# Shifting where the moving operands of matmuls begin in memory, modulo 256 bytes, against the weights

## The chip, the core and the metric

The kernel runs on one NeuronCore of a Trainium2 chip. TensorE (PE in the profile) multiplies; VectorE (DVE), ScalarE (ACT) and GpSimd (POOL) do the element-wise work; SyncE (SP) issues most of the DMAs. SBUF is the on-chip memory of 128 partitions that the operands lie in, and PSUM takes the matmuls' sums. The metric is the device time of one execution, in microseconds. The kernel before takes 3229.51 us (median of 3 runs, 3228.76 to 3231.86).

## What is computed

Two models run one after the other on a sequence of 256 tokens with 1024 features, all in float32. The first has two layers, each a mixer (a long convolution, a gated linear attention and a pooling branch, merged by three gates) and a gated feed-forward net of width 2816. The second has four layers (neighbourhood attention, a convolution module, a short gated convolution, attention again), each followed by a squared-ReLU MLP of width 4096; in its first three layers a second stream of 256 context tokens goes along. Cut to what matters:

```python
for i in range(2):                                   # first model
    h = _rms_norm(x, norm_mix_pre[i]); proj = h @ w_in[i]
    ...                                              # three branches, three gates
    x = x + _rms_norm(merged @ w_out[i], norm_mix_post[i])
    a, b = _split(_rms_norm(x, norm_ffn_pre[i]) @ ffn_w_up[i], (D_FF, D_FF))
    y = (gelu(_dwconv3_centred(a, ...)) * b) @ ffn_w_down[i]
    x = x + _rms_norm(y, norm_ffn_post[i])
for i in range(4):                                   # second model, streams x and ctx
    x = x + mod_l[:, 2] * mixer_i(modulate(rmsnorm(x, norm1_g[i]), ...))
    x = x + mod_l[:, 5] * (square(relu(m_l @ mlp_w1[i])) @ mlp_w2[i])
```

## The kernel before

**Layout.** Features lie on the 128 partitions and tokens along the free dimension, so a gemm has weights of 128 x 128 float32 as the stationary operand and 256 or 512 tokens as the moving one. In the first model and in the last layer's MLP and attention queries a moving operand has 256 columns (one stream); in the second model's layers 0 to 2 it mostly has 512 (both streams). At some tails and heads of layers 0 to 2 (`by_stream`, `head_tiles`) the two streams are done one after the other, with 256 columns each.

**Three matmuls for one.** Every float32 number is held as a rounded high part and a low part. `mm3` makes one product of three matmuls: high weights by high activations (line 142), high by low (147), low by high (148). Each matmul comes with its own weight load (LDWEIGHTS, PEld in the profile), which runs beside the matmul before it. A gemm over 1024 features is a chain of 8 contraction tiles, 24 matmuls, into one PSUM bank.

```python
i = nc.tensor.matmul(out, wh, xh, start=start, stop=False, skip_group_check=True)
...
    nc.tensor.matmul(out, wh, xl, start=False, stop=False, skip_group_check=True)
    nc.tensor.matmul(out, wl, xh, start=False, stop=stop, skip_group_check=True)
```

**Weights.** `load_w` fetches 1 MB of weights by SP's queue into `raw` (two buffers), ScalarE rounds them into `whi` (line 128) and VectorE takes the rest into `wlo` (line 130), 1024 elements a partition at a time, in rings of four buffers. A buffer is free again when PE is through with it.

**Moving operands.** `ah`, `al` (8 x 512 per partition) hold the normalized activations of every stage; the first model uses their first 256 columns as the gemms' operand and the other 256 for two of its branches (`branch`). `yph`, `ypl` are the third branch; `hh`, `hl` the operand of the feed-forward's down gemm and of `w_out`; `mhh`, `mhl` that of the MLPs' second gemm; `vh`, `vl`, `uh`, `ul`, `soh`, `sol` those of the output gemms of the attention, the convolution module and the short convolution; `Ph`, `Pl` the attention's weights by head, which move against `vh`, `vl` as stationary operand. In the value gemms (`w_v`, `att_v`) the roles are turned: `whi`, `wlo` move with 512 columns, and `ah`, `al` are stationary.

**Order.** A tile framework allots addresses and puts waits; each engine runs its instructions in program order. Pools are stacks: a tile that is put in front of another moves its address and nothing else. The mixer's steps (`STEPS`) and the attention's loop over pairs of heads leave VectorE and ScalarE work between gemms; gates, feed-forward nets and MLPs are long runs of gemms.

Of the kernel before, what the change touches and what calls it, by code (L numbers as in the profile page):

```python
# [11 lines left out]
F32R = mybir.dt.float32r  # L12
# [6 lines left out]
P = 128  # L19
T = 256  # L20
KD = 8
NL1 = 2
NL2 = 4
# [12 lines left out]

STEPS = (("h", 0), ("z", 0), ("h", 1), ("z", 1), ("h", 2), ("z", 2), ("h", 3), ("z", 3),
         ("p", 0), ("x", 0), ("x", 1), ("p", 1), ("g", 0), ("g", 1))


_VEC = {}
# [38 lines left out]
class Kern:  # L80
# [13 lines left out]
    def t(self, pool, tag, shape, dt=F32, bufs=None):  # L94
        kw = {} if bufs is None else {"bufs": bufs}
        return pool.tile(list(shape), dt, tag=tag, name=self.nm(tag), **kw)

    def ps(self, tag="mm", dt=F32):
        return self.psum.tile([P, 512], dt, tag=tag, name=self.nm(tag), bufs=self.psbufs[tag])
# [160 lines left out]
    def setup(self):  # L260
        nc, a = self.nc, self.a
        self.cp = self.pool("cp", bufs=1)
        self.wp = self.pool("wp", bufs=1)
        self.psbufs = {"mm": 2, "ko": 4, "mi": 1, "mo": 1}
        self.psum = self.pool("ps", bufs=1, space=PSUM)
        self.X = self.t(self.cp, "X", [P, 2, KD, T])
        self.vec = self.t(self.cp, "vec", [P, _NV])
        with self.tc.high_priority():
            self.ordered(self.vec[:, :NV1], a["vecs"][:, :NV1])
            self.ordered(self.X[:, 0, 0:4], a["x"][:, 0:4])  # L270
        self.ident = self.t(self.cp, "ident", [P, P])
        self.lead = [(self.X[:, 0, 4:8], a["x"][:, 4:8]), (self.ident, a["ident"])]
        self.ones = self.t(self.cp, "ones", [P, P])
        nc.vector.memset(self.ones, 1.0)
        self.inv = {}
        for nd in (P, DM):
            self.inv[nd] = self.t(self.cp, f"inv{nd}", [P, 2])
            nc.vector.memset(self.inv[nd], 1.0 / nd)
        self.mhalf = self.t(self.cp, "mhalf", [P, 4])
        nc.vector.memset(self.mhalf, -0.5)  # L280
        self.one1 = self.t(self.cp, "one1", [P, 1])
        nc.vector.memset(self.one1, 1.0)
        self.mod = [self.t(self.cp, f"mod{l}", [P, 2, 48]) for l in range(NL2)]
        self.sc = self.t(self.cp, "sc", [P, KD, 32])
        nc.vector.memset(self.sc, 0.0)
        nc.gpsimd.memset(self.mod[NL2 - 1], 0.0)
        self.mod_done = 0
        self.mroom = None
        self.mods = self.mod_bursts()

        self.main = self.pool("main", bufs=1)
        self.ah = self.t(self.main, "ah", [P, KD, 512], F32R)
        self.al = self.t(self.main, "al", [P, KD, 512], F32R)

    def silu_c(self):
        nc = self.nc
# [83 lines left out]
    def run(self, out):  # L380
        nc, a, X = self.nc, self.a, self.X
        with ExitStack() as st:
            self.f1 = self.pool("f1", st, bufs=1)
            with ExitStack() as mx:
                self.b1 = b1 = self.pool("mx", mx, bufs=1)
                self.mroom = b1, 2
                self.dft = self.t(b1, "dft", [P, 4, 2, P])
                self.cnt = self.t(b1, "cnt", [P, 4, 2, 8])
                self.smask = self.t(b1, "smask", [P, T])
                nc.vector.memset(self.smask, 1.0)  # L390
                nc.vector.memset(self.smask.rearrange("p (c t) -> p c t", t=P)[:, :, 0:1], 0.0)
                self.lmask = self.t(b1, "lmask", [P, P], U32)
                update = self.ffn(0, self.mixer(0, None))
                update = self.mixer(1, update)
            self.mp = self.pool("mix0", st, bufs=1)
            vs = self.att_v(0, 0)
            update = self.ffn(1, update, lambda: next(vs))
            norm = self.norm0
            acc = self.t(self.main, "sacc", [P, T], bufs=1)
            for m in range(KD):  # L400
                update(m)
                sq = acc if not m else self.t(self.main, "s2", [P, T], bufs=6)
                self.mark = nc.scalar.activation(sq, X[:, 0, m], AF.Square).ins
                if 0 < m < KD - 1:
                    nc.gpsimd.tensor_tensor(acc, acc, sq, ALU.add)
            self.norm_stream(norm, 0, [acc, sq])
            nxt = []
            self.attention(0, 0, norm, vs, True, self.behind(0, nxt))
        with ExitStack() as st:
            self.mp = self.pool("mlp0", st, bufs=1)  # L410
            norm = self.mlp(0, 512, nxt[0])
        for l in range(1, NL2):
            norm = self.layer2(l, norm)
        for k in range(0, KD, 2):
            eng = (nc.sync, nc.scalar)[k // 2 % 2]
            eng.dma_start(out[:, k : k + 2], X[:, 0, k : k + 2])
# [13 lines left out]
    def prenorm1(self, g, update=None):  # L430

        nc, X = self.nc, self.X
        xh, xl = self.ah[:, :, :T], self.al[:, :, :T]
        for k in range(KD):
            if update:
                update(k)
            gk = self.v(g, k)
            self.mark = nc.scalar.activation(xh[:, k], X[:, 0, k], AF.Copy, scale=gk).ins
            nc.vector.scalar_tensor_tensor(xl[:, k], X[:, 0, k], gk, xh[:, k].bitcast(F32), ALU.mult, ALU.subtract)  # L439
        acc = self.sumsq([X[:, 0, 2 * k : 2 * k + 2] for k in range(4)], self.main)  # L440
        rt, rp = self.rstd([q[:, j] for q in acc for j in range(2)], DM, self.main)
        r = self.t(self.main, "rs", [P, T], bufs=2)
        nc.scalar.copy(r, rp)
        return xh, xl, r, rt
# [66 lines left out]
    def branch(self, q, n=1):  # L511

        if q < KD:
            return tuple(x[:, q : q + n, T:] for x in (self.ah, self.al))
        return tuple(x[:, q - KD : q - KD + n] for x in self.yp)

    def filter_time(self, h, w3, tag):
# [36 lines left out]
    def mixer(self, i, update):  # L554
# [112 lines left out]
        for m in range(KD):  # L667
# [4 lines left out]
            for b in range(3):  # L672
                dst = psl[b // 2][:, b % 2]
                for k in range(KD):
                    wh, wl = lg[b]
# [37 lines left out]
                ctx = self.norm_context()  # L713
            if i + 1 == NL1 and m == KD - 1:
                for k in range(KD):
                    self.shift_split(self.norm0[0], k, 1, ctx[:, k])
            if m:
                out(*pend)
            pend = (m, mh, ml)
# [246 lines left out]
    def norm_open(self, l, which):  # L966

        nc, mod = self.nc, self.mod[l]
        s0 = 24 * which
        gs = self.t(self.main, "gs", [P, 2, 8], bufs=2)  # L970
        nc.vector.scalar_tensor_tensor(
            gs, mod[:, :, s0 + 8 : s0 + 16], 1.0,
            self.v(f"norm{which + 1}_g{l}", 0, 8)[:, None, :].to_broadcast([P, 2, 8]), ALU.add, ALU.mult,
        )
        return mod[:, :, s0 : s0 + 8], gs, self.ah, self.al

    def shift_split(self, sh, k, s, t):
        ah, al = (x[:, k, s * T : (s + 1) * T] for x in (self.ah, self.al))
        b = sh[:, s, k : k + 1]
        self.nc.scalar.activation(ah, t, AF.Identity, bias=b)  # L980
        self.nc.vector.scalar_tensor_tensor(al, t, b, ah.bitcast(F32), ALU.add, ALU.subtract)  # L981

    def norm_stream(self, norm, s, parts):
        nc, X = self.nc, self.X
        sh, gs, ah, al = norm
        _, rp = self.rstd(parts, DM, self.main)
        r = self.t(self.main, "rs", [P, T], bufs=2)
        nc.scalar.copy(r, rp)
# [1 line left out]
        for k in range(KD):  # L990
            t = self.t(self.main, "s2", [P, 512], bufs=6)[:, :T]
            nc.vector.scalar_tensor_tensor(t, X[:, s, k], gs[:, s, k : k + 1], r, ALU.mult, ALU.mult)
            self.shift_split(sh, k, s, t)

    def head_tiles(self, src, cnt, xh, xl, n, tag="ko", order=(0, 1)):

# [101 lines left out]
    def mlp(self, l, n, norm):  # L1098
        nc, a = self.nc, self.a
        _, _, mh, ml = norm  # L1100
        if l + 1 < NL2:
            self.spread_c()
        s1 = self.tiles(a["mlp_w1"][l])
        s2 = self.tiles(a["mlp_w2"][l])
        nxt = []
# [41 lines left out]
    def att_v(self, l, slot):  # L1147

        mp, a = self.mp, self.a
        v = [self.t(mp, tag, [P, 4, DM], F32R) for tag in ("vh", "vl")]  # L1150

        def weights(n2):
# [6 lines left out]
        def group(ws, n2, tts, tags):  # L1159
            pv = [self.ps(tag) for tag in tags]  # L1160
            for kk in range(KD):
                wh, wl = (w[:, kk % 2] for w in ws[kk // 2])
                for ps, tt in zip(pv, tts):
                    s = slice(tt * P, (tt + 1) * P)
                    self.mm3(ps, self.ah[:, kk, s], self.al[:, kk, s], wh, wl, kk == 0, kk == KD - 1)
            return lambda: [
                self.split(*(q[:, tt, n2 * 512 : (n2 + 1) * 512] for q in v), ps) for ps, tt in zip(pv, tts)
            ]
# [19 lines left out]
    def attention(self, l, slot, norm, vs, live, done):  # L1188
# [63 lines left out]

        def values(hp, S, st):
            nk = 4 if st == 0 else 2
            ph = []
            for h in range(2):
                Ph = self.t(mp, "Ph", [P, 4, T], F32R, bufs=2)
# [51 lines left out]
    def conformer(self, l, norm, done):  # L1309
# [103 lines left out]
        nc.gpsimd.tensor_tensor(r, var, self.mhalf, ALU.pow)  # L1413
        nc.vector.scalar_tensor_tensor(nm, mu, -1.0, r, ALU.mult, ALU.mult)
        rb, nb = self.spread(r, "mi"), self.spread(nm, "mm")
        uh = self.t(mp, "uh", [P, KD, 512], F32R)
        ul = self.t(mp, "ul", [P, KD, 512], F32R)
        for m in range(KD):
# [8 lines left out]
    def short(self, l, norm, done):  # L1427
        nc, a, mp = self.nc, self.a, self.mp
        _, _, ah, al = norm
        src = self.tiles(a["sc_win"])  # L1430
        W = T + 2
        oh = self.t(mp, "soh", [P, KD, 512], F32R)
        ol = self.t(mp, "sol", [P, KD, 512], F32R)
        for m in range(KD):
# [238 lines left out]
```

## Time and profile before

| | before |
|---|---|
| median of 3 runs | 3229.51 us (3228.76 to 3231.86) |
| profiled execution | 3229.86 us |
| its span (first to last instruction) | 3228.1 us |
| PE busy | 3122.4 us, 97% |
| DVE busy | 2140.7 us, 66% |
| ACT busy | 1498.2 us, 46% |
| mean granted clock of PE | 0.982 |

A matmul's record begins when its columns begin to enter; its end is modelled, so one record overlaps the next, and the pace of a run of matmuls is the distance from start to start. Busy time of PE is the union of these records.

### The profile page before, as it was taken

The numbers are of one execution on the slowest core, as the hardware profiler recorded it, in microseconds if no ns is written. First come the engines' busy times: TensorE is split into PE (matmuls) and PEld (weight loads), VectorE is DVE, ScalarE is ACT, GpSimd is POOL, SyncE is SP. The second block draws the span as 40 slices with busy tenths as digits, with TensorE's granted clock in tenths as the row PEclk, the third lists the DMA queues.
The fourth block names the chain that finished last, engine by engine and source line by source line (L and its number), as shares of the span: only waits on it lengthen the run. The fifth ranks groups of instructions, "written<-read, shape, count | busy, mean of one in ns | idle before, by whom it ended". The sixth has DMA issues, their size and how long they took to land.

```text
span 3228.1 us, 46918 instructions
## 1 busy us (share of the span) xinstructions
PE 3122.4 (97%) x18954; PEld 2707.5 (84%) x18954; DVE 2140.7 (66%) x3445; ACT 1498.2 (46%) x2371; POOL 226.6 (7%) x219
## 2 busy tenths in 40 slices
PE   8899999989999999999999899999999999999998
PEld 6699898889899778888886588888888888787898
DVE  6876666786776566898358869943547843446655
ACT  5344445444544576433346553333334333346654
POOL 0200000020101100000006500000000000110000
PEclk9899999999999999999999899999999999999999
DMA  8345565445454221575221137722234832222354
GB/s 287 121 163 183 178 227 200 163 145 182 163 183 157 92 79 46 173 238 189 96 88 66 40 109 236 236 98 92 92 105 157 299 105 92 97 92 95 121 183 144
DMA packets 81337, 469.12 MB, mean 145 GB/s; under 512 B 9364, under 2 KB 9802, under 8 KB 37088
## 3 DMA queue, kind: packets, MB, share of 16 engines
q1 hardware_dynamic: 78768, 460.01, 42.0%
q0 software_dynamic: 1328, 4.31, 0.4%
q8 instruction: 149, 2.44, 0.3%
q10 hardware_dynamic: 1024, 1.81, 0.2%
q14 instruction: 68, 0.56, 0.1%
HBM read 465.04 MB, written 1.05 MB: 144 GB/s over the span
## 4 chain that ended last, share of the span: by engine, by line
PE 65%; issue 23%; DVE 7%; ACT 2%; POOL 1%; DMA 1%; SPq 0%; POOLq 0%; DVEq 0%; ACTq 0%
PE ko L142 9%; PE ko L147 9%; PE mm L142 9%; PE ko L148 9%; PE mm L147 9%; PE mm L148 9%; DVE wlo L130 2%; ACT whi L128 1%; PE mm L1262 1%; PE mo L142 1%; PE mo L147 1%; PE mo L148 1%; DVE mm L1387 1%; PE mi L224 1%; POOL nms L228 1%
## 5 line engine op out<-in xcount | busy, mean ns | idle before, releaser
L128 ACT CAST whi<-raw 128x1024 fp32r<-128x1024 f32 (+2 forms) x676 | 699.1, 1037 | 1212.5 <-PE mm L147 677.8
L130 DVE TENSOR_TENSOR wlo<-raw,whi 128x1024 fp32r<-128x1024 f32 (+2 forms) x656 | 797.1, 1218 | 416.8 <-ACT whi L128 411.7
L142 PE MATMUL ko<-ah,whi 128*128 128x512 f32 (+1 forms) x1536 | 545.0, 356 | 3.7 <-ACT ah L980 3.0
L147 PE MATMUL ko<-al,whi 128*128 128x512 f32 (+1 forms) x1536 | 544.2, 355 | 1.3 <-DVE al L981 1.3
L148 PE MATMUL ko<-ah,wlo 128*128 128x512 f32 (+1 forms) x1536 | 543.4, 355 | 0.0
L142 PE MATMUL mm<-ah,whi 128*128 128x256 f32 (+1 forms) x1744 | 509.2, 292 | 23.2 <-DVE s L464 20.5
L148 PE MATMUL mm<-ah,wlo 128*128 128x256 f32 (+1 forms) x1744 | 505.2, 290 | 0.8 <-DVE wlo L130 0.8
L147 PE MATMUL mm<-al,whi 128*128 128x256 f32 (+1 forms) x1744 | 504.8, 289 | 0.4 <-DVE al L439 0.4
L142 PEld LDWEIGHTS mm<-ah,whi 128*128 128x128 f32 x1744 | 337.9, 194 | 44.0 <-issue 30.1
L147 PE MATMUL mm<-mhl,whi 128*128 128x512 f32 (+1 forms) x952 | 345.5, 363 | 0.3
L142 PE MATMUL mm<-mhh,whi 128*128 128x512 f32 (+1 forms) x952 | 345.3, 363 | 0.0
L148 PE MATMUL mm<-mhh,wlo 128*128 128x512 f32 (+1 forms) x952 | 345.0, 362 | 0.0
L148 PEld LDWEIGHTS mm<-ah,wlo 128*128 128x128 f32 x1744 | 337.5, 194 | 6.3 <-DVE wlo L130 1.8
L147 PEld LDWEIGHTS mm<-al,whi 128*128 128x128 f32 x1744 | 337.8, 194 | 5.8 <-issue 1.6
L142 PEld LDWEIGHTS ko<-ah,whi 128*128 128x128 f32 x1536 | 290.2, 190 | 45.2 <-ACT ah L980 3.7
L353 DVE SCALAR_TENSOR_TENSOR mjunk<-mraw,cb 128x1024 f32<-128x1024 f32 x256 | 312.7, 1222 | 20.1 <-DMA mraw<-in_mod_w_dram 14.6
L147 PEld LDWEIGHTS ko<-al,whi 128*128 128x128 f32 x1536 | 290.6, 189 | 41.2 <-DVE al L981 1.7
L148 PEld LDWEIGHTS ko<-ah,wlo 128*128 128x128 f32 x1536 | 290.4, 189 | 39.6 <-issue 0.2
L147 PEld LDWEIGHTS mm<-mhl,whi 128*128 128x128 f32 x952 | 178.3, 187 | 33.6 <-DVE mhl L205 1.5
L1022 DVE SCALAR_TENSOR_TENSOR X<-mm,mod,X 128x256 f32<-128x256 f32 x206 | 92.8, 479 | 171.2 <-PE mm L148 171.2
L142 PEld LDWEIGHTS mm<-mhh,whi 128*128 128x128 f32 x952 | 178.3, 187 | 32.2
L148 PEld LDWEIGHTS mm<-mhh,wlo 128*128 128x128 f32 x952 | 178.3, 187 | 32.0
(396 smaller groups left out, 5066.4 us busy)
## 6 DMA issues: line engine op xcount, KB each, us to landing
raw<-in_mlp_w_dram SPq DMA_DIRECT2D x128, 1024.0 KB, 4.9
mraw<-in_mod_w_dram SPq DMA_DIRECT2D x144, 512.0 KB, 4.3
raw<-in_w_in_dram SPq DMA_DIRECT2D x52, 1024.0 KB, 4.9
raw<-in_w_up_dram SPq DMA_DIRECT2D x44, 1024.0 KB, 4.9
mraw<-in_mod_w_dram SPq DMA_DIRECT2D x24, 1024.0 KB, 4.9
raw<-in_w_down_dram SPq DMA_DIRECT2D x22, 1024.0 KB, 4.9
raw<-in_na_qk_dram SPq DMA_DIRECT2D x16, 1024.0 KB, 4.8
raw<-in_w_br_dram SPq DMA_DIRECT2D x16, 768.0 KB, 4.3
```

The costliest lines, as they stand in the source:

```text
L128: nc.scalar.copy(hi[:, :step], raw[:, s])
L130: eng.tensor_tensor(lo[:, :step], raw[:, s], hi[:, :step].bitcast(F32), ALU.subtract)
L142: i = nc.tensor.matmul(out, wh, xh, start=start, stop=False, skip_group_check=True)
L147: nc.tensor.matmul(out, wh, xl, start=False, stop=False, skip_group_check=True)
L148: nc.tensor.matmul(out, wl, xh, start=False, stop=stop, skip_group_check=True)
L224: nc.tensor.matmul(*args, start=False, **kw)
L228: nc.gpsimd.tensor_tensor(y, x, self.mhalf[:, :nch], ALU.pow)
L353: nc.vector.scalar_tensor_tensor(junk, w, 1.0, self.cb[:, r], ALU.mult, ALU.mult, accum_out=mod[:, r, n : n + 1])
L1022: nc.vector.scalar_tensor_tensor(X[:, s, m], ps[:, sl], self.mod[l][:, s, 8 * gate + m : 8 * gate + m + 1], X[:, s, m], ALU.mult, ALU.add)
L1262: nc.tensor.transpose(pt[:, kt * P : (kt + 1) * P], S[2 * h + qt][:, kt * P : (kt + 1) * P], self.ident)
L1387: nc.vector.scalar_tensor_tensor(d, u[:, :, j : j + T], tap(j), d, ALU.mult, ALU.add)
```

## The change

Nothing is computed otherwise: the built program has the same instructions on every engine, in the same order and with the same waits. What differs is where tiles lie. The weights `whi` and `wlo` begin at 192 modulo 256 bytes in every contraction tile, before and after (a tile of weights is 512 bytes long, so this holds for each). Below, "at" means that a moving operand begins at the weights' place modulo 256, and "64 in front" that it begins 64 bytes before it.

| moving operand, columns | matmuls | before | after |
|---|---|---|---|
| `ah`, `al` of the first model, 256 | 5040 | at | 64 in front |
| `ah`, `al` of the last layer's MLP, 256 | 768 | at | 64 in front |
| `Ph`, `Pl` against `vh`, `vl`, 256 | 480 | at | 64 in front |
| `yph`, `ypl`, 256 | 192 | 128 from it | 64 in front |
| `mhh`, `mhl` of layers 0 to 2, 512 | 2088 | 64 in front | at |
| `vh` (layer 0), `soh`, `uh` and their low parts, 512 | 360 | 64 in front; `uh` 32 behind | at |
| `ah`, `al` of the second model, 512 | 3456 | at | at, but 64 in front for 384 of layer 0's attention |
| tails of layers 0 to 2: `mhh`, `vh`, `soh`, `uh`, 256 | 864 | 64 in front; `uh` 32 behind | at |
| heads of layers 0 to 2 and the last layer's queries: `ah`, `al`, 256 | 960 | at | at |
| `hh`; last layer's `mhh`, `vh`; 256 | 2400 | 64 in front | 64 in front |
| `whi`, `wlo` against `ah`, `al` as weights, 512 | 288 | at | 64 behind |

The last line is of the value gemms of the first model and of layer 0; those of the last layer stay. `operand` makes `ah` and `al` 64 bytes longer, with two views of each: `bh`, `bl` begin at its start, `ah`, `al` 64 bytes behind it. The first model, layer 0's attention and the last layer's MLP take `bh`, `bl`; all else takes `ah`, `al`.

```diff
+PADS = {("v", 0): 64, ("v", 3): 0, ("p", 0): 192, ("p", 3): 192, ("m", 0): 64, ("s", 0): 64, ("u", 0): 224,
+        ("h", 0): 64, ("h", 1): 64, ("h", 2): 64, ("h", 3): 0}
...
+    def pad(self, pool, n, i=0):
+        if n:
+            self.t(pool, f"pad{i}", [P, n // 4])
+    def operand(self, tag):
+        x = self.t(self.main, tag, [P, KD * 512 + 64], F32R)
+        return tuple(x[:, o : o + KD * 512].rearrange("p (k t) -> p k t", t=512) for o in (16, 0))
...
-        self.ah = self.t(self.main, "ah", [P, KD, 512], F32R)
-        self.al = self.t(self.main, "al", [P, KD, 512], F32R)
+        self.pad(self.main, 192)
+        self.ah, self.bh = self.operand("ah")
+        self.al, self.bl = self.operand("al")
+        self.pad(self.main, 64, 1)
...
-        xh, xl = self.ah[:, :, :T], self.al[:, :, :T]
+        xh, xl = self.bh[:, :, :T], self.bl[:, :, :T]
...
+        if l + which in (0, NL2):
+            return mod[:, :, s0 : s0 + 8], gs, self.bh, self.bl
         return mod[:, :, s0 : s0 + 8], gs, self.ah, self.al
...
+        self.pad(self.mp, PADS["h", l])
...
+        xh, xl = (self.ah, self.al) if l else (self.bh, self.bl)
+        self.pad(mp, PADS["v", l])
```

The other pads stand in the same way in front of the first pool of the mixers, of `Ph`, of `uh` and of `soh`.

## Rows read from the trace of the kernel before

**Rows 1.** The page: span, busy time by engine, and the chain that ended last.

```profile
span 3228.1 us, 46918 instructions
PE 3122.4 (97%) x18954; PEld 2707.5 (84%) x18954; DVE 2140.7 (66%) x3445; ACT 1498.2 (46%) x2371; POOL 226.6 (7%) x219
...
PE 65%; issue 23%; DVE 7%; ACT 2%; POOL 1%; DMA 1%; SPq 0%; POOLq 0%; DVEq 0%; ACTq 0%
```

**Rows 2.** Who waited for whom: us in total, times, longest us.

```profile
ACT whi L128 <- PE mm L147: 677.8, 283, 5.4
...
PE mm L142 <- DVE s L464: 20.5, 3, 11.6
...
PE mm L142 <- ACT whi L128: 11.0, 3, 7.8
```

**Rows 3.** Stretches: length, busy us (count) of PE, PEld, DVE, ACT, POOL; PEclk; DMA.

```profile
25.00:150.00 125.00, 117.18 (x785) 93.27 (x783) 92.72 (x178) 55.22 (x77) 14.44 (x19) 0.96 0.54 192
150.00:162.00 12.00, 5.51 (x25) 5.36 (x26) 11.16 (x18) 2.95 (x6) 6.80 (x6) 0.52 0.27 89
215.00:325.00 110.00, 108.03 (x864) 103.46 (x863) 71.06 (x100) 49.12 (x61) 0.72 (x1) 0.97 0.53 178
345.00:530.00 185.00, 182.28 (x1515) 175.80 (x1517) 126.12 (x173) 93.76 (x132) 0.00 (x0) 0.99 0.62 215
1345.00:1657.00 312.00, 312.00 (x1356) 253.94 (x1356) 220.90 (x333) 112.38 (x148) 0.00 (x0) 1.00 0.51 169
3060.00:3217.00 157.00, 156.71 (x1339) 155.91 (x1338) 91.53 (x115) 85.89 (x135) 0.00 (x0) 1.00 0.51 170
```

**Rows 4.** PE's groups by shape: count; busy us, mean ns; idle before, releaser.

```profile
L142 PE MATMUL mm<-ah,whi 128*128 128x256 f32 x1680 | 484.3, 288 | 23.2 <-DVE s L464 20.5 <-ACT whi L128 2.0 <-ACT ah L438 0.5
...
L147 PE MATMUL mm<-mhl,whi 128*128 128x512 f32 x696 | 274.4, 394 | 0.0
...
L142 PE MATMUL mm<-mhh,whi 128*128 128x256 f32 x256 | 71.0, 277 | 0.0
...
L142 PE MATMUL ko<-mhh,whi 128*128 128x256 f32 x144 | 40.4, 281 | 0.0
...
L147 PE MATMUL mi<-Pl,vh 128*128 128x256 f32 x128 | 38.8, 303 | 0.0
...
L142 PE MATMUL mo<-ah,whi 128*128 128x512 f32 x64 | 25.0, 391 | 0.0
...
L142 PE MATMUL mm<-yph,whi 128*128 128x256 f32 x64 | 18.2, 284 | 0.0
```

**Rows 5.** PE in time, last layer's MLP, 256 columns, operand at the weights' place.

```profile
3140.09 0.28 PE L147 MATMUL ko<-al,whi 128*128 128x256 f32 x1
3140.20 0.28 PE L148 MATMUL ko<-ah,wlo 128*128 128x256 f32 x1
...
3142.49 0.28 PE L142 MATMUL ko<-ah,whi 128*128 128x256 f32 x1
```

**Rows 6.** PE in time, the same MLP, 256 columns, operand 64 in front.

```profile
3160.03 0.28 PE L142 MATMUL mm<-mhh,whi 128*128 128x256 f32 x1
3160.14 0.28 PE L147 MATMUL mm<-mhl,whi 128*128 128x256 f32 x1
...
3162.41 0.28 PE L142 MATMUL mm<-mhh,whi 128*128 128x256 f32 x1
```

**Rows 7.** PE in time, layer 0's MLP, 512 columns, operand at the weights' place.

```profile
1420.04 0.39 PE L148 MATMUL ko<-ah,wlo 128*128 128x512 f32 x1
...
1422.99 0.39 PE L142 MATMUL ko<-ah,whi 128*128 128x512 f32 x1
```

**Rows 8.** PE in time, the same MLP, 512 columns, operand 64 in front.

```profile
1560.10 0.39 PE L148 MATMUL mm<-mhh,wlo 128*128 128x512 f32 x1
...
1562.90 0.39 PE L148 MATMUL mm<-mhh,wlo 128*128 128x512 f32 x1
```

**Rows 9.** PE in time, output gemm of the convolution module, 512 columns, 32 behind.

```profile
1880.05 0.40 PE L148 MATMUL ko<-uh,wlo 128*128 128x512 f32 x1
...
1884.48 0.39 PE L142 MATMUL ko<-uh,whi 128*128 128x512 f32 x1
```

**Rows 10.** PE in time, tail of layer 0's attention output, 256 columns, 64 in front.

```profile
1311.92 0.28 PE L142 MATMUL ko<-vh,whi 128*128 128x256 f32 x1
...
1313.45 0.28 PE L147 MATMUL ko<-vl,whi 128*128 128x256 f32 x1
```

More of the change, by code (lines that the diff above doesn't have):

```diff
@@ L386, in run @@
                 self.mroom = b1, 2
+                self.pad(b1, PADS["m", 0])
                 self.dft = self.t(b1, "dft", [P, 4, 2, P])
@@ L513, in branch @@
         if q < KD:
-            return tuple(x[:, q : q + n, T:] for x in (self.ah, self.al))
+            return tuple(x[:, q : q + n, T:] for x in (self.bh, self.bl))
         return tuple(x[:, q - KD : q - KD + n] for x in self.yp)
@@ L715, in mixer @@
                 for k in range(KD):
-                    self.shift_split(self.norm0[0], k, 1, ctx[:, k])
+                    self.shift_split(self.norm0, k, 1, ctx[:, k])
             if m:
@@ L974, in norm_open, with shift_split @@
         )
+        if l + which in (0, NL2):
+            return mod[:, :, s0 : s0 + 8], gs, self.bh, self.bl
         return mod[:, :, s0 : s0 + 8], gs, self.ah, self.al
-    def shift_split(self, sh, k, s, t):
-        ah, al = (x[:, k, s * T : (s + 1) * T] for x in (self.ah, self.al))
+    def shift_split(self, norm, k, s, t):
+        sh, _, *ops = norm
+        ah, al = (x[:, k, s * T : (s + 1) * T] for x in ops)
         b = sh[:, s, k : k + 1]
@@ L984, in norm_stream @@
         nc, X = self.nc, self.X
-        sh, gs, ah, al = norm
+        gs = norm[1]
         _, rp = self.rstd(parts, DM, self.main)
@@ L992, in norm_stream @@
             nc.vector.scalar_tensor_tensor(t, X[:, s, k], gs[:, s, k : k + 1], r, ALU.mult, ALU.mult)
-            self.shift_split(sh, k, s, t)
+            self.shift_split(norm, k, s, t)
     def head_tiles(self, src, cnt, xh, xl, n, tag="ko", order=(0, 1)):
@@ L1164, in group @@
                     s = slice(tt * P, (tt + 1) * P)
-                    self.mm3(ps, self.ah[:, kk, s], self.al[:, kk, s], wh, wl, kk == 0, kk == KD - 1)
+                    self.mm3(ps, xh[:, kk, s], xl[:, kk, s], wh, wl, kk == 0, kk == KD - 1)
             return lambda: [
@@ L1254, in values @@
             nk = 4 if st == 0 else 2
+            if not hp and not st:
+                self.pad(mp, PADS["p", l], 1)
             ph = []
@@ L1415, in conformer @@
         rb, nb = self.spread(r, "mi"), self.spread(nm, "mm")
+        self.pad(mp, PADS["u", 0])
         uh = self.t(mp, "uh", [P, KD, 512], F32R)
@@ L1431, in short @@
         W = T + 2
+        self.pad(mp, PADS["s", 0])
         oh = self.t(mp, "soh", [P, KD, 512], F32R)
```

## The prediction

> **What bounds the kernel now.** I read the page first, then the list of waits, then the busy time by stretch, and at last PE's own pace in single gemms. The page [rows 1] has PE busy for 97% of the span, and the chain that ended last runs 65% through PE's matmuls and 23% through "issue", time in which nothing in the profile held the next piece up; in the long gemm runs that is PE running its queue. DVE has 7% of that chain, ACT 2%. So a nanosecond taken off a matmul counts, if nothing else is right behind PE. The waits say that nothing is [rows 2]: ACT, which rounds the weights, stood 677.8 us in 283 waits for PE to give back a weight buffer, so weights lie ready before PE comes to them; PE stood only 11.0 us for a rounded weight, in 3 waits, and its longest sort of wait, for DVE in the mixers, is 20.5 us in 3. By stretch [rows 3], PE is busy 182.28 of 185 us in a feed-forward net, where DVE has 126.12, and 312.00 of 312 us in layer 0's MLP, where DVE has 220.90. Only the mixers' steps (93 of 125 us of DVE, in which PE still has 117) and the 12 us after them, with DVE at 11.16 and PE at 5.51, are places where another engine sets the time.
>
> So PE's pace is the matter, and the pace is not one number. In the last layer's MLP, the first gemm's operand begins at the weights' place: from the start at 3140.09 to that at 3142.49 there are 20 steps, 120.0 ns each [rows 5]. The second gemm of the same MLP has the same shape and weights from the same buffers, but its operand begins 64 bytes in front: 21 steps from 3160.03 to 3162.41, 113.3 ns each [rows 6]. With 512 columns it is the other way about: 13 steps of 226.9 ns at the weights' place [rows 7], 12 steps of 233.3 ns 64 in front [rows 8], and 19 steps of 233.2 ns 32 behind [rows 9]. The modelled lengths of the records say the same for whole groups of 256 columns [rows 4]: 288 ns at the weights' place, 277 for 64 in front, 284 for `yph`, which is 128 away. The kernel before has each width mostly at the worse of these places, so this trace holds the price of most of the change: about 6.5 ns a matmul for either width.
>
> **The change part by part.** Order, waits and instructions stay, so there is no queue that is passed and no new wait; the terms are counts times 6.5 ns, with the counts from the table of the change (`mm3` makes three matmuls of each of the groups' counts: 1680 is a third of 5040, 696 of 2088 [rows 4]).
>
> Gains with 256 columns: `ah` of the first model, 5040 x 6.5 = 32.8 us; of the last layer's MLP, 768 x 6.5 = 5.0; `Ph`, 480 x 6.5 = 3.1 (its place before is that of rows 5); `yph`, 192, for which the records' 284 against 288 and 277 put 4 to 5 ns in place of 6.5: 0.9. Gains with 512: `mhh` of layers 0 to 2, 2088 x 6.5 = 13.6; `vh`, `soh` and `uh`, 360 x 6.5 = 2.3. Together 57.7 us.
>
> Losses: the tails of layers 0 to 2 share tiles with operands of 512 columns and go to the worse place for 256. At full price that is 864 x 6.5 = 5.6 us; a tail of layer 0 ran at 117.7 ns though it lay 64 in front (13 steps from 1311.92 to 1313.45 [rows 10]), so some have less to lose, about 2.3 ns, and the bounds are 2.0 and 5.6; I take 5.6, since first halves of tails look like rows 6. Layer 0's queries and keys, 384 matmuls of 512 columns, go from rows 7's place to rows 8's: 2.5 us. The value gemms of the first model and of layer 0, 288 matmuls whose weights move against `bh`, get a place that no row shows, 64 behind. The nearest rows are 32 behind [rows 9] and the two ends of the pace, 6.5 ns apart; nothing excludes a gain, so the bounds are -1.9 and +1.9 us, and I take +1.0, toward rows 9. Together 9.1 us, and the net is 48.6 us of PE time.
>
> What of it reaches the end? Some stretches run at the lower clock (0.52 granted over 150 to 162 us [rows 3], where PE had been short of work); matmuls there may not feel the address, and a mean granted clock of 0.98 puts that at 1 us. The gates, feed-forward nets and MLPs have 3648 of the first 5040, and all of `mhh` and of the last layer; there PE is busy for 98% to 100% and DVE for 58% to 71% [rows 3]. With some 6 us off a feed-forward net's 185, DVE's 126.12 us are 70% of it; nothing else comes late, so these gains (23.7 + 13.6 + 5.0 = 42.3 us) arrive almost whole. The other 1392 of the 5040, 9.0 us, are the mixers' steps. There DVE has 32 us free of 125, so most passes, but the stops in front of DVE may grow by what PE gains ahead of them: I take a third off, 3 us, bounds 0 and 9. Layer 0's attention loop is a wash, `Ph` against its queries and keys. That leaves 48.6 - 1 - 3 = 44.6, say 45 us; with the bounds, 37 to 52. The profiled execution, 3229.86 us, has 1.8 us outside its span and lies 0.35 us from the median, so the median serves: 3229.5 - 45 = **3184.5 us**.
>
> A rule speaks against all of it. The Trainium skill says, in "TensorE: Matmul & The Clock Gate", "Step-by-step: what each phase is for", that PE has two independent SBUF read ports and that loading the next tile's weights takes no read bandwidth from the running matmul. By that rule the place of one against the other has no price, the sum is 0 and the time 3229.5. Rows 5 to 8 disagree: two widths, each with both places inside one MLP, 6.5 ns apart and in opposite directions.
>
> **The rivals.**
> *No effect.* The difference in rows 5 to 8 is not the place but something else that goes with the gemm: the PSUM bank's ring (`ko` against `mm`), or the eviction behind it. Then 3229.5 us. Against it: `mm` with `ah` has the longer records, `mm` with `mhh` the shorter ones [rows 4], so it isn't the bank; and an eviction that slows 256 columns would hardly quicken 512. 4%.
> *Another engine takes over.* PE's gain turns into waits, for rounded weights in the feed-forward nets or for DVE in the mixers and MLPs of layers 0 to 2. If only the gates, feed-forward nets and last MLP paid (3648 + 768 matmuls, 28.7 us) less the 9.1 us of losses, 20 us come through: 3210. For it: DVE at 71% with bursts. Against it: ACT's 677.8 us of waiting for PE. 14%.
> *Slower.* PE, quicker between its stops, runs out of work in the mixers, and the granted clock falls there more often. One such stretch, 150 to 162 us [rows 3], has 5.51 us of matmuls at about half speed, so costs about 2.8 us. To eat 45 us and 6.5 more takes 18 of them beyond those of now; it decides once DVE has nothing free in the steps, and it has 32 us of 125. About 3250. 2%.
> *More than forecast.* All passes, tails cost 2.0, the unseen place gains: 55 us or more, 3172. 5%.
>
> **How the numbers follow.** The forecast gets 75%. Its own bounds, 37 to 52 us, are 3177.5 to 3192.5. Two in ten may stay out, so the range reaches up for the better half of the second rival and down to the last: 3173 to 3203. A measurement of this kernel tells about 0.2%, 6.5 us, from no change. The forecast, the second rival and the last are all faster by more: 94%; the first rival is "same", 4%; slower 2%.
>
> **What would show it.** In the trace after, start-to-start in the gates and feed-forward nets at 113 to 114 ns, and in the MLPs' second gemm at 227; the tails and layer 0's queries slower by about 6; the value gemms somewhere from 220 to 234; DVE's busy time as it was; PE's waits for DVE in the mixers no more than a few us longer. Wrong it would be if the pace of `ah` with 256 columns stayed at 120 ns (then the place isn't the cause), or if the pace fell and PE's idle time grew by the same (then another engine was right behind it).

## The result and the profile after

The changed kernel takes 3187.62 us (median of 4 runs, 3179.97 to 3189.86) against 3229.14 us beside it, a ratio of 0.987 (0.9858 to 0.9882): 41.5 us faster, where 45 were forecast, and inside the range. Its profiled execution took 3185.85 us. The page of after, for [rows 1]: span, busy us and share by engine, and the chain that ended last.

```profile
span 3184.1 us, 46918 instructions
PE 3076.0 (97%) x18954; PEld 2677.8 (84%) x18954; DVE 2139.5 (67%) x3445; ACT 1498.8 (47%) x2371; POOL 226.8 (7%) x219
...
PE 64%; issue 23%; DVE 7%; ACT 3%; POOL 1%; DMA 1%; SPq 0%; POOLq 0%; DVEq 0%; ACTq 0%
```

The span is 44.0 us shorter, PE's busy time 46.4 us; DVE, ACT and POOL have what they had. So PE did the same matmuls in less time, and stands idle for 108.1 us in place of 105.7. In the numbering of after, `mm3` is at lines 155, 160 and 161 (142, 147 and 148 of before), and the weights are rounded at 141. The waits of after (who waited for whom: us, times, longest) answer to [rows 2]:

```profile
ACT whi L141 <- PE mm L160: 637.2, 281, 5.5
...
PE mm L155 <- DVE s L481: 20.8, 3, 11.7
...
PE mm L155 <- ACT whi L141: 11.9, 4, 8.2
...
PE ko L860 <- DVE gk L839: 2.1, 6, 0.6
```

ACT waits 40 us less for PE to give buffers back and still 637 us; PE's longest sort of wait for DVE and that for ACT are up by 0.3 and 0.9 us. Another sort of wait for DVE, for the tile `gk` in the mixers' steps, grew more; it was, before:

```profile
PE ko L843 <- DVE gk L822: 0.6, 2, 0.4
```

So no engine was right behind PE in the long runs of gemms, but DVE was close behind it in the steps.

Now the pace, PE in time of after: start, length of the record, line, operation. The last MLP's first gemm, 256 columns, now 64 in front, against [rows 5]; the second gemm of layer 0's MLP, 512 columns, now at the weights' place, against [rows 8]; the tail of layer 0's attention output, 256 columns, now at the place, against [rows 10]; layer 0's queries, 512 columns, now 64 in front.

```profile
3060.04 0.28 PE L160 MATMUL ko<-al,whi 128*128 128x256 f32 x1
...
3062.76 0.28 PE L160 MATMUL ko<-al,whi 128*128 128x256 f32 x1
...
1524.95 0.39 PE L160 MATMUL mm<-mhl,whi 128*128 128x512 f32 x1
...
1527.67 0.39 PE L160 MATMUL mm<-mhl,whi 128*128 128x512 f32 x1
...
1266.55 0.28 PE L155 MATMUL ko<-vh,whi 128*128 128x256 f32 x1
...
1268.71 0.28 PE L155 MATMUL ko<-vh,whi 128*128 128x256 f32 x1
...
1053.01 0.39 PE L155 MATMUL mo<-ah,whi 128*128 128x512 f32 x1
...
1057.91 0.39 PE L155 MATMUL mo<-ah,whi 128*128 128x512 f32 x1
```

24 steps of 113.3 ns, 12 of 226.7, 18 of 120.0 and 21 of 233.3. The rows of before named above hold for the first two. The matmuls of [rows 10] lie later in the tail; those shown here, and layer 0's queries, ran in before as follows, 18 steps of 113.3 and 21 of 226.7:

```profile
1294.99 0.28 PE L142 MATMUL ko<-vh,whi 128*128 128x256 f32 x1
...
1297.03 0.28 PE L142 MATMUL ko<-vh,whi 128*128 128x256 f32 x1
...
1083.30 0.39 PE L142 MATMUL mo<-ah,whi 128*128 128x512 f32 x1
...
1088.06 0.39 PE L142 MATMUL mo<-ah,whi 128*128 128x512 f32 x1
```

The four prices changed places: what ran at 120 runs at 113.3, what ran at 233.3 runs at 226.7, and the two groups that were given up pay the full difference here. (The stretch of [rows 10], at 117.7 before, had only some 2 ns to lose.) PE's groups by shape (count; busy us, mean ns of one record; idle before) show the same by whole groups, beside [rows 4]:

```profile
L155 PE MATMUL mm<-ah,whi 128*128 128x256 f32 x1680 | 474.2, 282 | 23.5 <-DVE s L481 20.8 <-ACT whi L141 1.6 <-DVE A L721 0.6
...
L160 PE MATMUL mm<-mhl,whi 128*128 128x512 f32 x696 | 270.9, 389 | 0.8 <-DVE mhl L218 0.8
...
L155 PE MATMUL ko<-mhh,whi 128*128 128x256 f32 x144 | 41.2, 286 | 0.0
...
L160 PE MATMUL mi<-Pl,vh 128*128 128x256 f32 x128 | 38.5, 301 | 0.0
```

Two of these say that something is left over. `mm<-ah` went from 288 to 282, not to the 277 of `mm<-mhh` in [rows 4]; and `mi<-Pl` moved by 2 ns, not by 11. The first is the main question of the experiments. It is seen in two gates of the same profile, the same gemm with `ah` 64 in front, in layer 0 and in layer 1:

```profile
249.65 0.28 PE L155 MATMUL mm<-ah,whi 128*128 128x256 f32 x1
...
251.01 0.28 PE L155 MATMUL mm<-ah,whi 128*128 128x256 f32 x1
...
745.00 0.28 PE L161 MATMUL mm<-ah,wlo 128*128 128x256 f32 x1
...
750.30 0.28 PE L161 MATMUL mm<-ah,wlo 128*128 128x256 f32 x1
```

12 steps of 113.3 ns in layer 0, 45 of 117.8 in layer 1, at the full clock in both (1.00 granted). All 575 matmuls of `ah` that can be followed between 692 and 794 us had this second pace.

### The profile page after: what moved, and what is told of

It is laid out like the page before. It is cut to its first block, busy times and chain, and to the rows that moved or that the text cites. A ratio compares the mean times of both kernels' runs of the same rounds, so it can differ in the third digit from the quotient of the medians.

```text
span 3184.1 us, 46918 instructions
## 1 busy us (share of the span) xinstructions
PE 3076.0 (97%) x18954; PEld 2677.8 (84%) x18954; DVE 2139.5 (67%) x3445; ACT 1498.8 (47%) x2371; POOL 226.8 (7%) x219
## 4 chain that ended last, share of the span: by engine, by line
PE 64%; issue 23%; DVE 7%; ACT 3%; POOL 1%; DMA 1%; SPq 0%; POOLq 0%; DVEq 0%; ACTq 0%
PE ko L155 10%; PE ko L160 10%; PE ko L161 9%; PE mm L155 9%; PE mm L160 8%; PE mm L161 8%; DVE wlo L143 2%; ACT whi L141 1%; PE mm L1288 1%; PE mo L155 1%; PE mo L160 1%; PE mo L161 1%; DVE mm L1413 1%; PE mi L237 1%; POOL nms L241 1%
## 5 line engine op out<-in xcount | busy, mean ns | idle before, releaser
L155 PE MATMUL mm<-ah,whi 128*128 128x256 f32 (+1 forms) x1744 | 499.1, 286 | 23.5 <-DVE s L481 20.8
L160 PE MATMUL mm<-al,whi 128*128 128x256 f32 (+1 forms) x1744 | 495.8, 284 | 0.4 <-DVE al L456 0.4
L161 PE MATMUL mm<-ah,wlo 128*128 128x256 f32 (+1 forms) x1744 | 495.1, 284 | 0.8 <-DVE wlo L143 0.8
L155 PEld LDWEIGHTS mm<-ah,whi 128*128 128x128 f32 x1744 | 330.9, 190 | 43.5 <-issue 30.1
L160 PEld LDWEIGHTS mm<-al,whi 128*128 128x128 f32 x1744 | 331.3, 190 | 6.0 <-issue 1.6
L161 PEld LDWEIGHTS mm<-ah,wlo 128*128 128x128 f32 x1744 | 330.4, 189 | 6.3 <-issue 1.8
L160 PEld LDWEIGHTS ko<-al,whi 128*128 128x128 f32 x1536 | 290.7, 190 | 40.4 <-DVE al L1002 0.8
```

## The experiments

All times of kernels below are medians of several runs beside the kernel before; the programs without the model ran once. Stretches are compared instruction by instruction with the profile of before and named by its times.

### Only `ah` put back

```diff
-        return tuple(x[:, o : o + KD * 512].rearrange("p (k t) -> p k t", t=512) for o in (16, 0))
+        return tuple(x[:, o : o + KD * 512].rearrange("p (k t) -> p k t", t=512) for o in (16, 16))
```

> The changed kernel with one part undone: both views of ah and al begin at the weights' place, so the first model and the last layer's MLP stream 256 columns from there again, and layer 0's attention its 512. Theory 'place': the 5808 matmuls of 256 columns go back to 120 ns from 113.4 (or 117.6 where they went so), 28 to 36 us slower than the changed kernel with 2.5 us back from layer 0's queries and keys: 3212 to 3222 us. Rival 'the gain came from the other pads or from luck': 3187 us as the changed kernel.

Measured: 3208.43 us (3206.57 to 3210.67; ratio 0.994, 0.9929 to 0.9952), against 3189.49 us (ratio 0.9875, 0.9861 to 0.989) of the changed kernel on the same chip. The place of `ah` is worth 19 us; at least 25 were expected, and the median lies below the range of 3212 to 3222. By whole groups in this kernel:

```profile
L155 PE MATMUL mm<-ah,whi 128*128 128x256 f32 x1680 | 483.2, 288 | 22.9 <-DVE s L481 20.6 <-ACT whi L141 1.8 <-ACT ah L455 0.5
...
L160 PE MATMUL mm<-mhl,whi 128*128 128x512 f32 x696 | 270.9, 389 | 0.0
```

`ah` is back at 288 and `mhl` stays at 389: each operand has its own price, and a place moved alone moves only its own gemms. Against the changed kernel's profile of that chip, the gates and feed-forward nets lose 20.0 us, the steps 3.0, the last MLP 3.2 and layer 0's attention gains 3.3; the rest, about 6 us the other way, lies in 0 to 25 and 128 to 160 us, where the two profiles differ in the clock (told further down). The granted clock of this kernel was 0.984 to 0.987 in its five runs, that of the changed kernel 0.981 to 0.985 in four on the same chip. So the difference isn't one profile's alone, and what part of it the place of `ah` brings about isn't shown.

### Only `mhh` put back

```diff
-        ("h", 0): 64, ("h", 1): 64, ("h", 2): 64, ("h", 3): 0}
+        ("h", 0): 0, ("h", 1): 0, ("h", 2): 0, ("h", 3): 0}
```

> The changed kernel with the other part undone: mhh and mhl of layers 0 to 2 lie 64 in front of the weights' place again. Theory 'place': 2088 matmuls of 512 columns at 233.3 instead of 226.8 ns, 13.6 us more, and 432 of 256 columns in the tails at 113.4 instead of 120, 2.8 us less: about 10.8 us slower than the changed kernel, 3196 to 3200 us. Rival 'in the MLPs PE waits for rounded weights or VectorE, so its pace there is free': no difference.

Measured: 3203.67 us (3190.07 to 3214.8; ratio 0.9924, 0.9905 to 0.9943), 14.2 us above the changed kernel. The three MLPs of layers 0 to 2 stand within 0.07 us of the kernel before, where the changed kernel on this chip had gained 4.57, 4.69 and 4.23 us: 13.5 us, the forecast's term of 13.6. The whole kernel was expected 10.8 us above the changed one, since its tails get their good place back (3196 to 3200 us); the median lies 4 us above that, inside the spread of the single runs. `mhh` with 512 columns has one pace and one price. This kernel's runs are 25 us apart, though its MLPs are steady; its profile has layer 1's gates at 117.8 ns, as the first profile of after had, and the changed kernel's profile on this chip had them at 113.3.

### The changed kernel again

> The changed kernel unaltered, for comparison on one chip. Expected 3180 to 3190 us. If the stretch of the second layer's gates (692 to 794 us in the profile after), all of whose 256-column matmuls went at 117.8 ns, depends on how the stream happens to be set off, this profile has other stretches at 117 to 118 ns than that one; if it goes by the place in the program, the same stretch is slow again.

> The changed kernel once more, beside the next one on the same chip. Both theories: 3180 to 3190 us, and somewhere in the profile a stretch of 256-column gemms with ah or hh at 117.2 to 117.8 ns from start to start beside stretches at 113.3 (569 + 160 matmuls in layer 1's gates in the first profile of it). If the slower pace belonged to that place in the program, it would stand at 692 to 794 us again; if it is chosen anew at every break in the stream, it may stand anywhere, or in no long stretch.

> The changed kernel for the third time, beside the next one on the same chip: 3180 to 3192 us, with some streams of 256 columns at 117.8 ns, at other places than in the first profile.

Measured: 3189.49, 3190.24 and 3186.52 us, single runs from 3179.38 to 3192.86. The gates of layer 1 gained 4.48, 3.84 and 3.51 us on the kernel before (1.40 in the first profile): in all three they ran near 113.3. The same 45 matmuls as above in layer 1's gates, in the first of these three profiles (120.0 ns before and with `ah` put back, 117.8 in the first profile of after, here 113.3):

```profile
749.68 0.28 PE L161 MATMUL mm<-ah,wlo 128*128 128x256 f32 x1
...
754.78 0.28 PE L161 MATMUL mm<-ah,wlo 128*128 128x256 f32 x1
```

But in two of these profiles about 200 matmuls of the last MLP's `mhh` ran at 117.8, which the first had at 113.4, and in every profile a part of the mixers' steps did. Of some 5600 matmuls of `ah` that can be followed, 1596, 1098, 985 and 779 lay at 116 ns or more in the four profiles. So the second pace has no place in the program: it is drawn anew.

### Sixteen places without the model

A program of its own: after a short wait, or behind one to three fp32 matmuls, come 48 matmuls in two chains, with the same pattern of operands as `mm3`, at each of 16 places, then the next stream. All streams write one PSUM buffer. VectorE has nothing to do, ScalarE one copy between streams.

```python
for c in range(2):
    for k in range(KD):                       # o: where the moving operand begins
        xs = [a[:, 512 * k + o : 512 * k + o + n] for a in (ah, al)]
        ws = [a[:, P * k : P * k + P] for a in w]
        for j, (a, b) in enumerate(((0, 0), (0, 1), (1, 0))):
            nc.tensor.matmul(ps[:, :n], ws[a], xs[b], ...)
```

> A program of its own, not the reference's work: it leaves the whole model out and only times streams of 48 matmuls (high and low parts as in the kernel) against 128x128 weights, with the moving operand begun at 16 places, 16 bytes apart, around a period of 256 bytes, with 256 columns (outputs ca to cp) and with 512 (da to dp). The place counted from the weights is 64 bytes at a, 192 (that is 64 in front) at i, 0 at m. Each stream is set off from the next by a wait for an eviction, of five lengths, or by one to three float32 matmuls. Theory 'the place against the weights sets the pace': 256 columns go at about 113.4 ns at i and 120 at m, 512 columns at 233 at i and 227 at m, the places between them in between. In streams ea, ee, ei, em (256 columns) and fa, fe, fi, fm (512) the same moving addresses go against weights that lie 64 bytes further on, so their places are 0, 64, 128, 192: by this theory ea goes like cm and em like ci, fa like dm and fm like di. Rival 'the moving operand's own address sets it': ea goes like ca, em like cm. Rival 'not the address but the surroundings in the kernel': all 16 places go alike. Theory of two modes: at 64 in front single streams go at either 113.4 or about 117.6 ns, and which one changes with what stood before the stream; rival: the 117.6 of the kernel is VectorE's or ScalarE's traffic, then no stream here, where both are idle, goes at 117.6.

> A program of its own that leaves the model out: the same streams of 48 matmuls as in the first of this kind, now with the moving operand begun every 4 bytes around the period of 256 (outputs gaa, gab, ... with 256 columns, haa, hab, ... with 512; the first is 64 behind the weights' place, every next one 4 bytes further on). Theory 'lines of SBUF that both reads walk over': the pace is a function of the place alone with steps at 16 or 32 bytes; the place 112 behind, where all eight streams of 256 columns went at 113.8 to 114.2 ns, keeps one pace here too, and 64 in front again shows two. If 112 behind shows 117 to 118 here as well, its eight alike were luck, and there is no steadier place than 64 in front.

Measured, mean step of each stream without its first ones, in ns (8 streams of 256 columns, 2 of 512, at each place; places behind the weights', modulo 256):

| place | 256 columns | 512 columns |
|---|---|---|
| 0 | 119.8 to 120.0 | 227.4 |
| 16 | 113.3 in five, up to 118.7 in three | 231.7 |
| 64 | 117.8 | 228.8 |
| 112 | 113.8 to 114.3; 113.3 from the twelfth step on | 231.0 and 226.7 |
| 128 | 118.6 to 120.0 | 232.4 |
| 192 (64 in front) | 113.3 to 113.5 in six, 117.8 in two | 233.3 |
| the other ten | 116.6 to 120.1 | 230.0 to 236.7 |

PE's groups of that program (count; busy us, mean ns of a record) at 0 (`cm`), 64 behind (`ca`), 64 in front (`ci`), 112 (`cd`), and with 512 columns 64 in front (`di`), at 0 (`dm`) and 64 behind (`da`):

```profile
L55 PE MATMUL cm<-ah,wh 128*128 128x256 f32 x128 | 37.0, 289 | 3.3 <-ACT junk L59 2.2 <-ACT junk L61 1.1
L55 PE MATMUL ca<-ah,wh 128*128 128x256 f32 x128 | 36.6, 286 | 0.0
L55 PE MATMUL ci<-ah,wh 128*128 128x256 f32 x128 | 36.3, 284 | 3.3 <-ACT junk L59 2.2 <-ACT junk L61 1.1
L55 PE MATMUL cd<-ah,wh 128*128 128x256 f32 x128 | 36.2, 283 | 0.0
...
L55 PE MATMUL di<-ah,wh 128*128 128x512 f32 x32 | 12.9, 402 | 0.9 <-ACT junk L59 0.9
L55 PE MATMUL dm<-ah,wh 128*128 128x512 f32 x32 | 12.7, 397 | 0.9 <-ACT junk L59 0.9
L55 PE MATMUL da<-ah,wh 128*128 128x512 f32 x32 | 12.6, 395 | 0.7 <-ACT junk L61 0.4 <-ACT junk L59 0.4
```

With the operands where they were and a second set of weights 64 bytes further on, the numbers went with the place against the weights, not with the operand's own address: 119.8, 117.8, 118.6 and 113.3 (one of four 117.8) at 0, 64, 128 and 192. So it isn't the bank of PSUM, an eviction, a busy VectorE or traffic of a DMA; the rival of the operand's own address and that of the surroundings are out. And both paces of 64 in front appear with all else idle. The theory's places between the two weren't in between: 112 behind is as quick as 64 in front. Every stream there begins with six to ten steps of 114 to 122 ns and then keeps 113.3.

The finer program bears the two main places out: 112 behind had one pace again (113.3, in four of four streams), 64 in front two (113.3 in three, 117.8 in one). Its theory of steps at 16 or 32 bytes fell: the pace changes from one multiple of 4 to the next, and places that are no multiple of 16 bytes were all slower than the best of these, 115.5 to 123.3 ns (one stream 129.8), and with 512 columns 228.7 to 240. By the Trainium skill's "TensorE: Matmul & The Clock Gate", "Step-by-step: what each phase is for", the weight load takes no read bandwidth from the running matmul. By that rule one would expect one pace at all places, and the measured 113.3 to 120 ns decide against it. Why the place of one read against the other costs time, no run shows.

### What draws the second pace

> A program of its own, the model left out: streams of 48 matmuls of 256 columns, 8 of each sort. Streams ra to rf have both parts of the operand 64 bytes in front of the weights' place, and begin with no other matmul (ra) or with an fp32 matmul of 64, 128, 256, 384 or 512 columns (rb to rf). Streams sa to sj put the high and the low part at different places: 64 in front and 112 behind (sa), 112 and 64 in front (sb), 64 in front and 16 behind (sc), 16 and 64 in front (sd), both 16 (se), 112 and 16 (sf), 16 and 112 (sg), 64 in front and at the place (sh), 64 in front and 64 behind (si), both 112 (sj). Theory: which of the two paces (113.3 or 117.8 ns) a stream at 64 in front takes is fixed in its first steps, by how its start falls; then both appear in ra to rf, each for the whole stream, and the sort of lead shifts their shares (in the model 62 streams with a first step of 220 to 224 ns ran at 113.3, 26 with one of 225 to 227 ns at 117.8). If a lead or a pair of places gives 113.3 in 8 of 8, the slower pace can be avoided. Rival: the pace belongs to the moment of the chip; then neighbouring streams share it whatever their lead, and no sort has 8 of 8 but by luck.

Streams of 48 at 64 in front, 8 of each sort, without or with an fp32 matmul of a given width ahead:

```diff
+        if lead:
+            nc.tensor.matmul(ps[:, :lead], flat[:, 0:128], flat[:, 512 : 512 + lead], start=True, stop=True)
```

Measured: with no lead, or one of 64 or 128 columns, 24 of 24 streams came to 113.3. With 256, 384 or 512 columns, streams ran at 117.8 and 113.3 in strict turn, 12 and 12. The streams of one sort differ in the length of ScalarE's copy ahead of them: the slow ones came behind 96 and 200 columns, the quick ones behind 64 and 160, so that turn and copy can't be told apart here. Two neighbours of `rd` (256 columns ahead), PE in time:

```profile
175.34 0.28 PE L55 MATMUL rd<-ah,wh 128*128 128x256 f32 x1
...
177.46 0.28 PE L55 MATMUL rd<-ah,wh 128*128 128x256 f32 x1
...
182.05 0.28 PE L55 MATMUL rd<-ah,wh 128*128 128x256 f32 x1
...
184.43 0.28 PE L55 MATMUL rd<-ah,wh 128*128 128x256 f32 x1
```

18 steps of 117.8 ns, and 7 us later 21 of 113.3. A pace that changes with each stream, and in the same order for three sorts, isn't the moment of the chip: what stands ahead of a stream decides, and a stream keeps what it has drawn. In the model it can be read from the first step behind an fp32 matmul. Over five profiles with `ah` or `hh` 64 in front, all 81 streams whose first step was 220 to 224 ns went on at 113.3, all 29 with 225 to 227 ns at 117.8. That is a sign, not a cause: other starts (a first step of 201 ns) went either way, and in the program of 16 places a stream of 117.8 began with 222. What fixes a stream's start to a few ns wasn't found. High and low part at two different places (eight pairs) never ran at 113.3 throughout. Both parts at 112 behind came to 113.3 in eight of eight, both at 16 behind in seven (118.7 in one).

### 112 behind in place of 64 in front

```diff
-    return tuple(... for o in (16, 0))
+    return tuple(... for o in (40, 4))        # bh, bl now 112 bytes behind the weights' place
```

The last layer's `mhh` went there too; `hh`, `yph` and `Ph` stayed.

> The changed kernel with the 256-column operands of the first model and of the last MLP (ah, al, and the last layer's mhh, mhl) at 112 bytes behind the weights' place in place of 64 in front; layer 0's queries and keys go to 112 behind with 512 columns, the value gemms' weights to 112 in front. hh, yph, Ph stay 64 in front. Theory: 64 in front has two paces, 113.3 and 117.8 ns, 112 behind has one, 113.8 to 114.2 (streams without the model). Then no stretch of ah runs near 117.8, and the pace is 113.8 throughout: against the first profile of the changed kernel 569 + about 1000 matmuls in the mixers' steps gain 3 to 4 ns each (-5 to -6 us), the other 4200 lose 0.5 (+2), the value gemms +1.3: 0 to 5 us faster than the changed kernel, and less spread from run to run. Rival: the slower pace is a matter of the chip's moment (a refresh, a neighbour) and not of the place: then 117.8 appears here too, the pace is 113.8 at best, and the time is 1 to 4 us longer than the changed kernel's.

Measured: 3184.67 us (3184.17 to 3193.58), against 3190.24 (3184.09 to 3192.86) of the changed kernel on the same chip; their profiled executions, 3184.47 and 3184.09, are equal, and so are the kernels within what was measured; nor do the single runs of the one lie closer together (9.4 us against 8.8). Half of the theory held: no stretch of `ah` ran near 117.8, and the steps had means of 113.9 to 114.8 ns against 113.9 to 116.6 at 64 in front. But the nets took 1.9 and 1.6 us longer than in the first profile of after. In them `hh` (64 in front) and `ah` (112 behind) alternate, and each return to `ah` costs about a dozen steps of 120 ns, as here with 10; the streams of the program without the model began in the same way at this place:

```profile
480.30 0.29 PE L155 MATMUL mm<-ah,whi 128*128 128x256 f32 x1
...
481.50 0.28 PE L160 MATMUL mm<-al,whi 128*128 128x256 f32 x1
```

A last kernel took the nets back to 64 in front by a third view of `ah`, and left the rest at 112.

> The kernel with ah at 112 behind, but the feed-forward nets (2112 matmuls) back at 64 in front, where hh also lies; the mixers' steps, the gates and the last MLP stay at 112 behind. In the profile with ah at 112 behind, each return from hh (64 in front) to ah cost about ten steps at 120 ns, and the feed-forward nets took 1.9 and 1.6 us longer than in the changed kernel. Theory: these 3.4 us come back (345 to 530 and 845 to 1025 us of before: 178.2 and 173.1 us, as in the changed kernel), and the steps keep their mean of 114.4 to 114.8 ns; 1 to 5 us faster than the changed kernel on the same chip. Rival: the mean of the steps is again a draw, and the two kernels are equal within 2 us.

Measured: 3195.87 us (3189.85 to 3197.35), against 3186.52 for the changed kernel beside it. It is no fair trial. The third view shares 20 elements of each contraction tile with the half that the branches use, so part of the first model works on overwritten numbers. Layer 0's net came back to 178.5 us and its pace to 113.4, as the theory has it; layer 1's net took 178.0 in place of 173.1. Of these 4.9 us PE stood 3.5 in three waits for weights (2.2 for `whi`, 1.3 for `wlo`) that the changed kernel doesn't have there. So the theory is neither borne out nor refuted, and whether both gains can be had together stays open.

## Why the prediction was right, step by step

**What bounds the kernel, and the price.** PE's pace was the matter, and 6.5 ns a matmul was the price for either width. *No effect* fell with the first rows of after, *another engine takes over* with the waits and PE's idle time, which grew by 2.4 us in all; for *slower* by the clock there is no sign (0.986 granted in the mean, 0.982 before).

**The terms.** Measured by stretches of the first profile of after, or where a stretch mixes terms by counts times the mean step:

| term | forecast, us | came |
|---|---|---|
| gates and feed-forward nets, `ah` | -23.7 | -21.2, of it some -2.5 by the clock |
| mixers' steps, `ah` | -9.0 + 3.0 | -5.5 |
| `mhh`, layers 0 to 2 | -13.6 | -12.1 |
| last MLP, `ah` | -5.0 | -4.1 |
| `Ph` | -3.1 | -1.0 |
| tails | +5.6 | about +4.4 |
| layer 0's queries and keys | +2.5 | +2.3 |
| value gemms | +1.0 | about +0.5 |
| `vh`, `soh`, `uh`, 512 | -2.3 | -2.1 |
| `yph` | -0.9 | -0.6 |

That the forecast's 44.6 lies within 1 us of the span's 44.0 is in part luck. The terms as measured come to some 39 us, 2.5 of it the clock's, so the forecast was some 8 us too high; the other 5 us of the span come from stretches that ran at a higher clock than before (128 to 160 and 1025 to 1065 us above all). The medians say the same: 41.5 us here, and 38.4, 35.5 and 40.4 in the three later comparisons with the kernel before, each on one chip. The range held all of them, the narrower bounds of 37 to 52 not the 35.5. (The upper of these isn't the sum of the prediction's own terms: no stops, tails at 2.0 and a gain at the unseen place make 54.) Three of the steps were wrong in their reason or size.

*Gates and nets.* The gates of layer 0 gave 6.34 us, of which 2.54 came in the kernel with `ah` back as well: PE's clock stood at 0.97 there before ([rows 3], 215 to 325) and at 1.00 after. Without that gift the term is 18.7 against 23.7. The larger part of the gap is the second pace: 729 matmuls of layer 1's gates (569 of `ah`, 160 of `hh` behind them, which had been quick before) at some 4.2 ns more, 3.1 us. The last 2 us aren't settled; the pace of the nets before, 119.6 to 119.7 with `ah` put back, is a part of them. The prediction had [rows 10] before it, a tail at 117.7 ns though it lay 64 in front, and took it only as "less to lose" there. It was the one row that showed the second pace of the very place that 6480 matmuls were to be sent to, and it should have been a bound of the gain: with a quarter of them at 117.8, some 7 us.

*The mixers' steps.* The 3 us were taken off for stops in front of DVE that grow, and 3.5 went. The three longest stops didn't grow (20.8 us against 20.5), but shorter ones did, as the line for `gk` above shows. Over the same work in both profiles (25 to 128, 162 to 215, 552 to 650 and 665 to 712 us of before) PE stood idle for 4.6 us before and 6.6 after; in the three other profiles of the changed kernel it was 7.7, 6.7 and 7.5. So 2 to 3 us went as forecast. The term that was left out is the second pace again: the steps ran at 115.3 to 116.6 ns in the mean, since every one of their short streams draws, and 1392 matmuls at 116 in place of 113.3 are 3.8 us. The two together are more than the 3.5 that went; a higher clock in 650 to 692 us (1.5 us gained there, 0.1 in the next profile) hid a part. The cause was right and its size about right, but a second loss of the same size was missing.

*`Ph`.* Its place before was the same as in rows 5, so it got the same 6.5 ns. Its pace was 118.7 before and is 116.7 after; its streams are short and against other weights (`vh`). The records in [rows 4] already had it apart, at 303 ns where the others had 288, and its price should have been bounded from 0.

*`mhh`, the last MLP.* The size was right: 13.5 us on another chip. In the first profile two stops in front of late operands stood in the way (PE idle for 0.77 and 0.85 us); such stops come in some profiles and not in others. The last MLP's first dozens of matmuls run at half clock, where the place has no price (below).

*The losses.* The tails and the value gemms came in their bounds, layer 0's queries and keys near their 2.5. The value gemms, whose place no row showed, had a median step of 229 ns against 227 before, half of what was taken for them; the program of sixteen places has 228.8 for 512 columns at 64 behind.

## What to carry to other kernels

Where PE is busy throughout, look at the step from start to start of each kind of matmul, by width and by where its moving operand begins against its weights modulo 256 bytes; two gemms of one kernel that have the same shape and weights give the price, and moving a tile costs some padding and no instruction. For these float32r matmuls of 128 rows the good places were the weights' own for 512 columns and 64 in front or 112 behind for 256. Read several stretches of the same place before you multiply: a place may have two paces.

## What the runs showed that was not expected

**Two paces at one place.** At 64 in front, 256 columns run at 113.3 or at 117.8 ns a step, fixed at the start of a stream and held for as long as 575 matmuls. Four profiles of one kernel had 14% to 28% of the `ah` matmuls at 116 ns or more; at 4.4 ns each that is 3 to 7 us. It isn't shown how much of the 13 us by which its single runs differ comes from this: the profile with the most of them (1596) took 3185.85 us, that with 1098 took 3190.04.

**At half clock the place has no price.** The last MLP's first matmuls, PE in time, of after (64 in front) and then of the kernel with `ah` put back (at the place), and PE in those stretches (length; busy; PEclk; DMA share; GB/s):

```profile
2996.24 0.41 PE L160 MATMUL ko<-al,whi 128*128 128x256 f32 x1
2996.46 0.41 PE L161 MATMUL ko<-ah,wlo 128*128 128x256 f32 x1
2996.67 0.41 PE L155 MATMUL ko<-ah,whi 128*128 128x256 f32 x1
...
2995.00:3000.00 5.00, 4.78 (x22) 0.50 0.23 98
```

```profile
3011.85 0.41 PE L160 MATMUL ko<-al,whi 128*128 128x256 f32 x1
3012.07 0.41 PE L161 MATMUL ko<-ah,wlo 128*128 128x256 f32 x1
3012.28 0.41 PE L155 MATMUL ko<-ah,whi 128*128 128x256 f32 x1
...
3010.80:3014.00 3.20, 3.17 (x15) 0.50 0.21 87
```

Both take 0.43 us for two steps at a granted clock of 0.50, the lower of the two levels (1.2 GHz); after a stop of 1.52 us PE came back to work there. Over the two profiles before and after, the steps of `ah` with 256 columns in the first model at this clock have the same median, 213 ns (79 steps at the place, 51 in front). The 6.5 ns of the full clock aren't seen there, which bears out the 1 us that the prediction set aside for such stretches in kind.

**The clock moves stretches by more than a term of the sum.** 128 to 160 us took 3.4 us less than before in the first profile of after, and 0.0 less in the second; 1025 to 1065 gained 2.4, 0 to 25 lost 1.9. Such differences come and go between executions of one kernel and between kernels, so a stretch with low clock in either profile says nothing about an edit of 3 us.
